# Query product of an attention layer on two float16 parts, with its weights read once more ahead for a scale, and all readings ahead rounded to bfloat16 by the transfer

## The chip, the cores and the metric

One core of a Trainium2 chip. The metric is the device time of one launch in microseconds (us); the kernel before was run three times, with a median of 1736.61 us (1736.53 to 1737.1).

## The reference

Two layers of a small diffusion transformer on 256 tokens x and 256 context tokens, width 2048, branch width 4096, all in float32. Layer 0 has a Fourier branch, layer 1 an attention branch. Cut to what matters here:

```python
def _attention_branch(h, hc, w_in, sink, rows, cols, need_ctx):
    q, k, v, z = jnp.split(h @ w_in, [D_BRANCH, D_BRANCH + kvw, D_BRANCH + 2 * kvw], axis=-1)
    kc, vc = jnp.split(hc @ w_in[:, D_BRANCH:D_BRANCH + 2 * kvw], 2, axis=-1)
    ...
    q = _axial_rope(q.reshape(b, n, ATTN_Q_HEADS, ATTN_HEAD_DIM), rows, cols)
    ...
    y = jnp.moveaxis(o, 0, 1).reshape(b, n, D_BRANCH) * jax.nn.silu(z)

for i in range(DEPTH):
    shift, scale, gate = jnp.split((jax.nn.silu(c) @ ada_w[i] + ada_b[i])[:, None, :], 3, axis=-1)
    h = _rmsnorm(x, norm_g[i]) * (1 + scale) + shift
    ...
    x = x + gate * (y @ w_out[i])
    if need_ctx:
        xc = xc + gate_c * (yc @ w_out[i])
return _rmsnorm(x, final_g)
```

The query product is the first 4096 columns of `h @ w_in`: 256 x 2048 by 2048 x 4096.

## The kernel before

**Products on two parts.** Every large product is made of three matmuls (mm3, L144 to L147): with w and x each split into a high and a low part, high times high, high times low, low times high. There are two ways of splitting a 128x1024 piece of weights. half_split (L69) rounds to the reduced fp32r on ACT (L66) and subtracts on DVE (L67); the parts are 4 bytes an element and take two slots of the pool ws. split16 (L134) multiplies by a power of two and rounds to float16 on ACT (L137) and forms the low part on DVE (L138); the parts share one slot of ws, but the scale must be known before the first piece is split, so that float16 does not overflow or lose its low bits.

**Readings ahead.** The scale of a weight matrix comes from the sum of its squares, so the matrix is read once ahead of the product that uses it. scan_loads (L831) reads layer 0's output weights wo0, scan_loads1 (L816) the key/value weights wkv and layer 1's output weights; loads2 in the key/value stage reads the rest of these. GpSimd (POOL) issues the loads, 128x512 float32 each into slots of the pool act (128x1024 into tiles pz in loads2); scan_sums (L826 to L829) squares them on ACT and adds the rows into a column of scn. half_scale, h1_bound and h1_scale turn the columns into power-of-two scales; h1_bound sends two columns through DRAM so that each partition gets the values of all.

**Stages, by the profile's time.** Opening and layer 0's Fourier product to about 326 us; layer 0's gate product to 657 (b = 0 to 31, 48 matmuls each); its output product to about 996 (i = 0 to 31, 48 matmuls of 128x512 each; step i first splits its two weight pieces, then issues readings, then goes on with the adaptive weights); key/value product 1002 to 1084; the query product, layer 1's gate product and attention, woven into each other by a list of units (emit_unit), to about 1590; layer 1's output product to the end. The query product takes the x half of the layer's input from hx1 (fp32r, two parts); the key/value product takes x and context from hz (float16, two parts).

**Order around the change.** Every engine works in the order of its instruction list. ada_jobs (L769 to L797) multiplies the adaptive-norm weights by a broadcast row: each step loads a tile zr on the queue of SP (L787) and a tile wa on POOL's queue (L790), and reduces each on DVE (L792). So a wa is issued behind the readings that stand ahead of it on POOL, and on DVE its reductions stand between the low parts (L138) of the output product's weights. In the output product ada_rate says how many of these steps go with step i, w_rate how many double readings of wkv and of layer 1's output weights.

Of the kernel before, what the change touches and what calls it, by code (L numbers as in the profile page):

```python
# [14 lines left out]
ALU = mybir.AluOpType  # L15
# [17 lines left out]
def tile_dit(ctx: ExitStack, tc: tile.TileContext, a: dict, out: bass.AP):  # L33
# [776 lines left out]
    ek, upk, dnk, kw = (keepc[:, c : c + 1] for c in range(4))  # L810
# [3 lines left out]
    scans1 = iter(range(52))  # L814

    def scan_loads1(n):  # L816
        for j in [next(scans1) for _ in range(n)]:
            for q in range(2):
                t = act()
                c = (j % 2 * 2 + q) * 512  # L820
                nc.gpsimd.dma_start(t, wst[j // 2][:, c : c + 512])
                c = j * 2 + q
                c += 80 if c < 28 else -28
                pend.append((t, scn[:, c : c + 1]))
# [6 lines left out]
    def scan_loads(n):  # L831
        for j in [next(scans) for _ in range(n)]:
            for q in range(2):
                t = act()
                c = (j % 2 * 2 + q) * 512
                nc.gpsimd.dma_start(t, a["wo0"][j // 32, j % 32 // 2][:, c : c + 512])
                c = j * 2 + q - 64 * (j >= 40)
                pend.append((t, scn[:, c : c + 1]))
# [5 lines left out]
    def half_sum(sw):  # L844
        return [col_sum(scn[:, sw * 16 : sw * 16 + 64])] + [col_sum(scn[:, 80:108])] * (sw == 0)
# [13 lines left out]
    with tc.tile_pool(name="yp", reuse_waits="tile", bufs=32) as ypool:  # L859
# [39 lines left out]
        if True:  # L899
# [44 lines left out]
            for b in range(4, NB):  # L944
# [28 lines left out]
                scan_loads((2 if b % 3 else 1) if b < 28 else 0)  # L973
            out0[0] = True
# [29 lines left out]
        hbd = dram.tile([P, 2], F32, name="hbd")  # L1004
        hb1 = []

        def h1_bound():
            m, c = h_bound(gs1, sh1, False), tiny(F32, 4, "t4")
            V.tensor_copy(c[:, 0:1], m)
            for i, q in ((2, slice(80, 108)), (3, slice(0, 4))):  # L1010
                V.tensor_reduce(c[:, i : i + 1], scn[:, q], axis=AX.X, op=ALU.add)
            V.tensor_tensor(c[:, 1:2], c[:, 2:3], c[:, 3:4], op=ALU.add)
            nc.gpsimd.dma_start(hbd, c[:, 0:2])
            hb1.append(act())
            nc.gpsimd.dma_start(hb1[0][:, 0:N], hbd.rearrange("(o p) c -> o (p c)", o=1).broadcast_to([P, N]))

        def h1_scale():
            v = hb1[0][:, 0:N].rearrange("p (n c) -> p c n", c=2)
# [7 lines left out]
            V.tensor_reduce(s, v[:, 1], axis=AX.X, op=ALU.add)  # L1026
            V.tensor_scalar(kw, s, 2.0**-70, None, op0=ALU.max)
            V.tensor_scalar(kw.bitcast(I32), kw.bitcast(I32), 24, 23, op0=ALU.logical_shift_right, op1=ALU.logical_shift_left)
# [798 lines left out]
```

## Time and profile before

| | before |
|---|---|
| median of three runs | 1736.61 us |
| the profiled execution's own time | 1736.42 us |
| its span, first to last instruction | 1734.6 us |
| HBM read / written | 419.30 MB / 12.59 MB |
| HBM traffic over the span | 249 GB/s |
| POOL's DMA queue (q0): packets, MB, share of 16 engines | 47344, 125.58, 22.7% |
| SP's DMA queue (q1): packets, MB, share of 16 engines | 197568, 335.60, 59.3% |
| mean granted TensorE clock | 0.998 |

How to read the profile: PE is TensorE's matmuls, PEld its weight loads (which overlap), DVE VectorE, ACT ScalarE, POOL GpSimd, SP the engine that issues most loads. In the row of slices each digit is the busy share in tenths of one fortieth of the span. A group is line, engine, operation, output<-inputs (partitions x elements, type), xcount | busy us, mean ns of one | idle time of the engine just before them and what ended it. A wait row names the waiting engine with its line, then what it waited for: us in total, times, the longest. Line numbers are those of the kernel of the profile.

### The profile page before, as it was taken

The numbers are of one execution on the slowest core, as the hardware profiler recorded it, in microseconds if no ns is written. First come the engines' busy times: TensorE is split into PE (matmuls) and PEld (weight loads), VectorE is DVE, ScalarE is ACT, GpSimd is POOL, SyncE is SP. The second block draws the span as 40 slices with busy tenths as digits, with TensorE's granted clock in tenths as the row PEclk, the third lists the DMA queues.
The fourth block names the chain that finished last, engine by engine and source line by source line (L and its number), as shares of the span: only waits on it lengthen the run. The fifth ranks groups of instructions, "written<-read, shape, count | busy, mean of one in ns | idle before, by whom it ended". The sixth has DMA issues, their size and how long they took to land. (4 is left out here: it accounts for less than half of the span.)

```text
span 1734.6 us, 28325 instructions
## 1 busy us (share of the span) xinstructions
PE 1703.1 (98%) x10379; PEld 1129.7 (65%) x10379; DVE 1373.2 (79%) x2390; ACT 1103.8 (64%) x2111; POOL 276.0 (16%) x429
## 2 busy tenths in 40 slices
PE   6999999999999999999999999999999999999997
PEld 4679999644444444446444654788888888876464
DVE  5779888798676787778689686888898989887755
ACT  5545555477777765464435397777787778777643
POOL 0001111211221204301420121300000000050001
PEclk9999999999999999999999999999999999999999
DMA  9998999869898968985997497489989899988643
GB/s 393 417 362 257 273 272 268 308 246 330 323 305 306 324 243 331 395 302 221 363 358 277 149 341 253 146 198 224 258 229 212 235 237 236 227 220 290 218 170 121
DMA packets 249195, 469.94 MB, mean 271 GB/s; under 512 B 171392, under 2 KB 171792, under 8 KB 222176
## 3 DMA queue, kind: packets, MB, share of 16 engines
q1 hardware_dynamic: 197568, 335.60, 59.3%
q0 software_dynamic: 47344, 125.58, 22.7%
q10 hardware_dynamic: 4144, 6.95, 1.2%
q8 instruction: 81, 1.33, 0.3%
q14 instruction: 58, 0.48, 0.1%
HBM read 419.30 MB, written 12.59 MB: 249 GB/s over the span
## 5 line engine op out<-in xcount | busy, mean ns | idle before, releaser
L67 DVE TENSOR_TENSOR wl<-raw,wh 128x1024 fp32r<-128x1024 f32 x152 | 188.4, 1256 | 43.1 <-ACT wh L66 33.0
L146 PE MATMUL ps<-act,wf 128*128 128x512 f16 x512 | 194.0, 379 | 0.0
L66 ACT CAST wh<-raw 128x1024 fp32r<-128x1024 f32 x152 | 157.3, 1046 | 57.6 <-PE ps L146 38.2
L147 PE MATMUL ps<-act,wf 128*128 128x512 f16 x512 | 191.1, 379 | 0.0
L145 PE MATMUL ps<-act,wf 128*128 128x512 f16 x512 | 189.8, 379 | 0.6 <-ACT wf L137 0.2
L145 PE MATMUL ps<-y,wf 128*128 128x512 f16 x448 | 169.8, 379 | 0.8 <-ACT wf L137 0.8
L146 PE MATMUL ps<-y,wf 128*128 128x512 f16 x448 | 169.8, 379 | 0.0
L145 PEld LDWEIGHTS <-wf 128*128 128x128 f16 x960 | 93.7, 98 | 113.4 <-ACT wf L137 4.2
L147 PEld LDWEIGHTS <-wf 128*128 128x128 f16 x960 | 93.9, 98 | 113.1
L147 PE MATMUL ps<-y,wf 128*128 128x512 f16 x448 | 164.9, 379 | 0.0
L146 PEld LDWEIGHTS <-wf 128*128 128x128 f16 x960 | 93.9, 98 | 109.0
L137 ACT ACTIVATE wf<-raw,nrm 128x1024 f16<-128x1024 f32 x56 | 63.5, 1145 | 131.4 <-PE ps L147 74.5
L145 PE MATMUL ps<-h,wh 128*128 128x256 f32 x512 | 144.4, 282 | 0.0
L146 PE MATMUL ps<-h,wh 128*128 128x256 f32 x512 | 142.7, 279 | 0.0
L147 PE MATMUL ps<-h,wl 128*128 128x256 f32 x512 | 142.6, 279 | 0.0
L1506 ACT ACTIVATE p<-ps,mx 128x512 f32<-128x512 f32 x128 | 87.8, 687 | 67.1 <-DVE mx L1502 64.7
L138 DVE SCALAR_TENSOR_TENSOR wf<-raw,tn,wf 128x1024 f16<-128x1024 f32 x64 | 79.8, 1282 | 42.6 <-ACT wf L137 42.6
L829 ACT ACTIVATE act<-act 128x512 f32<-128x512 f32 x178 | 109.4, 616 | 5.7 <-DMA act<-in_wo 4.4
L146 PE MATMUL ps<-wl,h 128*128 128x512 f32 x256 | 101.4, 396 | 0.0
L147 PE MATMUL ps<-wh,h 128*128 128x512 f32 x256 | 101.2, 395 | 0.0
L145 PEld LDWEIGHTS ps<-h,wh 128*128 128x128 f32 x512 | 96.1, 188 | 7.1 <-issue 5.5
L145 PE MATMUL ps<-wh,h 128*128 128x512 f32 x256 | 100.0, 402 | 0.0
(430 smaller groups left out, 4645.0 us busy)
## 6 DMA issues: line engine op xcount, KB each, us to landing
raw<-in_wz SPq DMA_DIRECT2D x64, 1024.0 KB, 6.3
raw<-in_awp SPq DMA_DIRECT2D x32, 1024.0 KB, 12.7
zr<-in_adw SPq DMA_DIRECT2D x64, 512.0 KB, 6.7
wa<-in_adw POOLq DMA_DIRECT2D x64, 512.0 KB, 6.3
act<-in_wo POOLq DMA_DIRECT2D x128, 256.0 KB, 7.4
raw<-in_wo SPq DMA_DIRECT2D x32, 1024.0 KB, 8.2
raw<-in_wq SPq DMA_DIRECT2D x32, 1024.0 KB, 5.8
raw<-in_wu SPq DMA_DIRECT2D x32, 1016.0 KB, 7.1
```

The lines of the kernel that those rows point to most:

```text
L66: last_cast[0] = S.copy(h, src).ins
L67: last_sub[0] = eng.tensor_tensor(l, src, h.bitcast(F32), op=ALU.subtract).ins
L137: last_cast[0] = S.activation(w[:, 0], src, AF.Copy, scale=up).ins
L138: last_sub[0] = V.scalar_tensor_tensor(w[:, 1], src, up, w[:, 0], op0=ALU.mult, op1=ALU.subtract).ins
L145: PE.matmul(o, wh, xh, start=start, stop=False)
L146: PE.matmul(o, wh, xl, start=False, stop=False)
L147: return PE.matmul(o, wl, xh, start=False, stop=stop).ins
L829: S.activation(t, t, AF.Square, accum_out=c)
L1506: S.activation(pt[hh, tb], so[hh, tb], AF.Exp, bias=mx[:, hh, tb : tb + 1], scale=-1.0, accum_out=sm[:, hh, tb : tb + 1])
```

## The change

The query product gets split16 with a scale upq, and the float16 parts hz as its input instead of hx1 (which stays for layer 1's gate product). The x half of hz therefore moves to eight tiles hzx of the pool act that live until the last query unit. The scale dnq that undoes upq is put into the Squares of the norm of q and into the rope table. For upq the query weights wq are read once more ahead, 64 loads of 128x1024: scan_loadsq issues one with each b from 4 to 27 and two with b = 28 to 31 of the gate product (32), and the others in the output product by q_rate. And every reading ahead now is one load of 128x1024 into a bfloat16 tile sn; source and destination differ in type, so the transfer rounds. Of wo0 and wkv that is half as many loads as before, each of twice the source. The diff's core:

```diff
+    qsn = c32.rearrange("p k c -> p (k c)")[:, 0:64]
+
+    def scan_load(src, j, col):
+        t = actp.tile([P, 1024], BF16, tag="act", name="sn")
+        c = j % 2 * 1024
+        nc.gpsimd.dma_start(t, src[:, c : c + 1024])
+        pend.append((t, col))
+
+    def scan_loadsq(n):
+        for j in [next(scansq) for _ in range(n)]:
+            scan_load(a["wq"][j // 8, j // 2 % 4], j, qsn[:, j : j + 1])
 
     def scan_loads1(n):
         for j in [next(scans1) for _ in range(n)]:
-            for q in range(2):
-                t = act()
-                c = (j % 2 * 2 + q) * 512
-                nc.gpsimd.dma_start(t, wst[j // 2][:, c : c + 512])
...
+            c = j + 64
+            scan_load(wst[j // 2], j, scn[:, c : c + 1])
...
     def scan_loads(n):
         for j in [next(scans) for _ in range(n)]:
-            for q in range(2):
-                t = act()
-                c = (j % 2 * 2 + q) * 512
-                nc.gpsimd.dma_start(t, a["wo0"][j // 32, j % 32 // 2][:, c : c + 512])
...
+            scan_load(a["wo0"][j // 32, j % 32 // 2], j, scn[:, j : j + 1])
...
                 scan_loads((2 if b % 3 else 1) if b < 28 else 0)
+                scan_loadsq(1 if b < 28 else 2)
...
+        q_rate = {**{i: 2 for i in range(6)}, **{i: 1 for i in (10, 11, 12, 13, 17, 18, 19, 20, 21, 23, 25)}, **{i: 3 for i in (14, 15, 16)}}
-        hbd = dram.tile([P, 2], F32, name="hbd")
+        hbd = dram.tile([P, 3], F32, name="hbd")
...
+            V.tensor_reduce(c[:, 2:3], qsn, axis=AX.X, op=ALU.add)
...
+            for c, up_, dn_ in ((1, upk, dnk), (2, upq, dnq)):
...
             scan_loads1(w_rate.get(i, 0))
+            scan_loadsq(q_rate.get(i, 0))
...
-                z2 = kvp.tile([P, 1024], F16, tag="hz", name="hz", bufs=16)
+                if k % 2 == 0:
+                    zx.append(actp.tile([P, 1024], F16, tag="act", name="hzx"))
+                z2 = zx[k // 2][:, k % 2 * 512 : k % 2 * 512 + 512], kvp.tile([P, 512], F16, tag="hz", name="hz", bufs=16)
...
-                    t = kvp.tile([P, 1024], F32, tag="pz", name="pz", bufs=4)
+                    t = kvp.tile([P, 1024], BF16, tag="pz", name="pz", bufs=8)
...
+                        V.tensor_scalar(rope, rope, dnq, None, op0=ALU.mult)
...
-                    S.activation(act(), oq[tb], AF.Square, accum_out=sq[:, tb, 0:1])
+                    S.activation(act(), oq[tb], AF.Square, scale=dnq, accum_out=sq[:, tb, 0:1])
...
-                return half_split(raws1[src], i % 2)
+                return split16(raws1[src], i % 2, upq) if kind == "q" else half_split(raws1[src], i % 2)
...
-                            pe_last[0] = mm3(o[tb], hx1[k][:, tb * P : (tb + 1) * P], hx1[k][:, N + tb * P : N + (tb + 1) * P], wh[:, q], wl[:, q], k == 0, k == KT - 1)
+                            t = hz[k][0]
+                            pe_last[0] = mm3(o[tb], t[:, tb * P : (tb + 1) * P], t[:, N + tb * P : N + (tb + 1) * P], wh[:, q], wl[:, q], k == 0, k == KT - 1)
```

The first place is POOL's list at the start of layer 0's output product, between two loads of wa (the adaptive weights, in_adw); in_wo is layer 0's output weight, x2 means twice in a row. Before:

```order
L790 DMA wa<-in_adw 128x1024 x5
L836 DMA act<-in_wo 128x512 x21
L790 DMA wa<-in_adw 128x1024
L836 DMA act<-in_wo 128x512 x9
L790 DMA wa<-in_adw 128x1024
L836 DMA act<-in_wo 128x512 x6
L821 DMA act<-in_wkv 128x512 x2
L836 DMA act<-in_wo 128x512 x4
L821 DMA act<-in_wkv 128x512
L790 DMA wa<-in_adw 128x1024
```

And in the changed kernel, behind the wa that is the last of the five above (in_wq is the query weight):

```order
L790 DMA wa<-in_adw 128x1024
L821 DMA sn<-in_wq 128x1024 x2
L821 DMA sn<-in_wo 128x1024 x2
L821 DMA sn<-in_wq 128x1024 x2
L821 DMA sn<-in_wo 128x1024 x2
L821 DMA sn<-in_wq 128x1024 x2
```

The pairs go on so up to the next wa. Between the two wa stand 21 loads in both kernels, of 256 KB before and of 512 KB of source now, 11 of them of wq.

The second place follows in the changed kernel: behind nine more loads and a wa, the eleven loads and the two blocks of xT (the tokens, to which the product is added) ahead of the next wa. There stood 13 loads of 128x512 before (the 6, 2, 4 and 1 above), and the two xT came behind that wa and the next:

```order
L790 DMA wa<-in_adw 128x1024
L821 DMA sn<-in_wo 128x1024 x2
L821 DMA sn<-in_wkv 128x1024
L821 DMA sn<-in_wq 128x1024
L821 DMA sn<-in_wo 128x1024 x2
L821 DMA sn<-in_wkv 128x1024
L821 DMA sn<-in_wq 128x1024
L821 DMA sn<-in_wo 128x1024 x2
L821 DMA sn<-in_wq 128x1024
L1066 DMA act<-in_xT 128x512 x2
L790 DMA wa<-in_adw 128x1024
```

After three more loads in both kernels comes the wa whose reductions stand in the third place; from the first wa to it there are 46 readings before, 44 in the changed kernel.

The third place is DVE at step i = 7 of the output product: the reductions of zr and wa (ISA rows) and the low part wf of the step's weights. In the changed kernel:

```order
L792 ISA zr_7630,acc_4144<-zr_7630,cb_6331 128x1024
L792 ISA acc_4144 128x1
L792 ISA junk_4143,acc_4144<-wa_7634,cb_6331 128x1024
L792 ISA acc_4144 128x1
L138 SCALAR_TENSOR_TENSOR wf_7768<-raw_7766,nrm_101,wf_7768 128x1024
L792 ISA wa_7634,acc_4144<-wa_7634,cb_6331 128x1024
```

Nothing moved on DVE here: before, the same rows stand in the same order (with other buffer numbers), wf directly behind the first reduction of the second wa.

41 lines of the change are left out of this document (18 added, 23 removed).

## The prediction

> **What bounds the kernel now.** I read the page's busy shares and slices first, then what PE waits for, then each stage by itself.
>
> ```profile
> PE 1703.1 (98%) x10379; PEld 1129.7 (65%) x10379; DVE 1373.2 (79%) x2390; ACT 1103.8 (64%) x2111; POOL 276.0 (16%) x429
> PE   6999999999999999999999999999999999999997
> DMA  9998999869898968985997497489989899988643
> ```
>
> PE is busy 98% of the span, and in all slices but the first and the last. So a stage is as long as its matmuls; another engine or a transfer costs time only where it makes PE wait. The waits of PE from 1085 to 1600 us (the query stage and attention), then from 330 to 1085 us:
>
> ```profile
> PE ps L146 <- DVE wl L67: 1.5, 2, 1.1
> PE ps L145 <- ACT wh L66: 0.5, 1, 0.5
> PE ps L145 <- ACT wf L137: 0.9, 2, 0.8
> ```
>
> That is 2 us of waiting for weights in 515 us, and 0.9 us in the 755 us ahead of it. How much cover there is shows in the stretches (length, then busy PE, PEld, DVE, ACT, POOL, then clock, DMA share, GB/s): layer 0's gate product, its output product, and two parts of the query and attention stage.
>
> ```profile
> 370.00:660.00 290.00, 290.00 (x1393) 132.11 (x1392) 227.17 (x401) 211.50 (x446) 58.69 (x111) 1.00 0.85 302
> 660.00:957.00 297.00, 296.23 (x1368) 142.16 (x1367) 233.56 (x355) 146.22 (x290) 75.54 (x142) 1.00 0.86 324
> 1112.00:1350.00 238.00, 237.06 (x1762) 196.22 (x1762) 212.60 (x394) 184.64 (x360) 12.14 (x9) 1.00 0.91 225
> 1350.00:1500.00 150.00, 150.00 (x1133) 124.93 (x1130) 133.10 (x253) 114.62 (x230) 4.66 (x4) 1.00 0.90 228
> ```
>
> The granted clock is 1.00 everywhere. The first two stretches are where the change adds reading, and their DMA engines are 85 and 86% busy already; the third and fourth are where the query product changes, with DVE 89% busy in both.
>
> **The query product (the gain).** Its matmuls are these three groups, 256 each, 768 together:
>
> ```profile
> L146 PE MATMUL ps<-wl,h 128*128 128x512 f32 x256 | 101.4, 396 | 0.0
> L147 PE MATMUL ps<-wh,h 128*128 128x512 f32 x256 | 101.2, 395 | 0.0
> L145 PE MATMUL ps<-wh,h 128*128 128x512 f32 x256 | 100.0, 402 | 0.0
> ```
>
> Matmuls overlap, so the price of one is the distance of their starts, not the 396 ns. From the timeline (start, duration), two rows 33 matmuls apart in the query product, and two rows 20 matmuls apart in the key/value product, which has the form that the query product gets (two float16 parts, 512 columns):
>
> ```profile
> 1180.10 0.40 PE L146 MATMUL ps<-wl,h 128*128 128x512 f32 x1
> 1187.80 0.40 PE L146 MATMUL ps<-wl,h 128*128 128x512 f32 x1
> ...
> 1039.63 0.38 PE L146 MATMUL ps<-wf,hz 128*128 128x512 f16 x1
> 1043.95 0.38 PE L145 MATMUL ps<-wf,hz 128*128 128x512 f16 x1
> ```
>
> 7.70/33 = 0.2333 us against 4.32/20 = 0.2160 us. The count of matmuls stays at three a pair, so the gain is 768 × 0.0173 = **13.3 us**. It is there only if the split keeps up: 64 pieces go from half_split to split16.
>
> ```profile
> L66 ACT CAST wh<-raw 128x1024 fp32r<-128x1024 f32 x152 | 157.3, 1046 | 57.6 <-PE ps L146 38.2 <-PE ps L147 12.1 <-DVE acc L792 3.9
> L137 ACT ACTIVATE wf<-raw,adab 128x1024 f16<-128x1024 f32 x50 | 56.1, 1141 | 34.9 <-PE ps L147 15.5 <-PE ps L146 10.1 <-DMA raw<-in_wo1b 3.4
> L67 DVE TENSOR_TENSOR wl<-raw,wh 128x1024 fp32r<-128x1024 f32 x152 | 188.4, 1256 | 43.1 <-ACT wh L66 33.0 <-issue 5.9 <-PE ps L147 2.7
> L138 DVE SCALAR_TENSOR_TENSOR wf<-raw,adab,wf 128x1024 f16<-128x1024 f32 x50 | 67.2, 1363 | 27.3 <-ACT wf L137 27.3
> ```
>
> ACT gets 64 × 95 ns = 6.1 us more, DVE 64 × 107 ns = 6.8 us. DVE's 345.7 of 388 us in the two stretches become 352.5 in some 375, or 94%: under the end, so I cost the split at nothing, with the rest as a rival. One weight slot instead of two for each piece lets the split run further ahead, which speaks for this. The scale on the Squares, one multiplication of the rope table (128x256) and five one-column steps of the scale are a dozen short instructions off PE's way: nothing.
>
> **The readings on ACT.** A reading of 128x512 costs ACT one Square; for the 128x1024 form I take the nearest row, a Square of that size that writes bfloat16.
>
> ```profile
> L829 ACT ACTIVATE act<-act 128x512 f32<-128x512 f32 x178 | 109.4, 616 | 5.7 <-DMA act<-in_wo 4.4 <-DMA act<-in_wkv 1.3
> L81 ACT ACTIVATE sq<-raw 128x1024 bf16<-128x1024 f32 x52 | 54.2, 1046 | 0.0
> ```
>
> Gate product: 80 readings become 72 long ones, 72 × 1.046 − 80 × 0.616 = +26 us, so ACT goes from 211.5 to about 238 of 290. Output product: 98 become 81, +24 us, 146 to 170 of 297. Both fit, cost nothing.
>
> **The readings on the DMA queues (the loss).** POOL issues fewer of them (178 become 153 of all), each of twice the source: a row of 4096 bytes is read and 2048 are written. The trace of before has no transfer that changes the type, so its price must be bounded. By the bytes written it is that of the old 256-KB load, by the bytes read twice that, and by read and written together three times. The place where it decides is the start of the output product, where the DMA engines are full (10-us stretches, same columns):
>
> ```profile
> 658.00:668.00 10.00, 10.00 (x48) 4.51 (x46) 9.56 (x15) 5.31 (x13) 6.77 (x13) 1.00 0.86 311
> 668.00:678.00 10.00, 10.00 (x48) 4.55 (x47) 7.96 (x10) 10.00 (x23) 4.98 (x10) 1.00 1.02 388
> 678.00:688.00 10.00, 10.00 (x48) 4.56 (x47) 2.06 (x3) 1.70 (x3) 2.68 (x5) 1.00 1.02 392
> 688.00:698.00 10.00, 10.00 (x48) 4.48 (x46) 7.92 (x12) 5.97 (x12) 6.96 (x13) 1.00 0.95 320
> 698.00:708.00 10.00, 10.00 (x48) 4.55 (x47) 8.95 (x13) 5.97 (x12) 4.69 (x9) 1.00 1.03 404
> 708.00:718.00 10.00, 10.00 (x48) 4.57 (x47) 4.15 (x6) 4.83 (x11) 2.83 (x6) 1.00 1.02 402
> 718.00:728.00 10.00, 10.00 (x48) 4.51 (x46) 8.67 (x14) 3.73 (x7) 3.93 (x8) 1.00 1.02 396
> ...
> 771.00:781.00 10.00, 10.00 (x48) 4.58 (x47) 3.78 (x4) 7.84 (x16) 0.53 (x1) 1.00 0.51 182
> 781.00:791.00 10.00, 10.00 (x48) 4.52 (x47) 9.91 (x17) 5.97 (x12) 3.15 (x6) 1.00 0.32 96
> ```
>
> A full share moves about 402 GB/s. POOL's queue takes the readings and the adaptive weights wa in order, and DVE works in order: its reduction of wa (L792) stands ahead of the low part wf (L138) that PE needs. Step i of the output product is 48 matmuls, 48 × 0.2157 = 10.35 us, from the 657.9 of the first row below. On DVE:
>
> ```profile
> L145 PE MATMUL ps<-y,wf x448: 379/379/389, 657.9 to 970.2; 128*128 128x512 f16 x150
> ...
> 723.96 1.23 DVE L792 CUSTOM_DVE_ANT_0 junk<-wa,cb 128x1024 f32<-128x1024 f32 x1 [1.26 <-DMA wa<-in_adw]
> 725.11 0.08 DVE L792 DVE_READ_ACCUMULATOR2_ANT acc<- 128x1 f32 x1
> 725.11 1.28 DVE L138 SCALAR_TENSOR_TENSOR wf<-raw,nrm,wf 128x1024 f16<-128x1024 f32 x1
> ```
>
> This wf belongs to the first half of i=7, which PE reaches at 657.9 + 7 × 10.35 = 730.3; it is done at 726.4. The slack is 4 us, and the wa ahead of it was late already (DVE idled 1.26 us). From 658 us to that wa POOL issues 46 readings before and 44 after (its two orders are shown with the change), and after also two xT blocks of 256 KB that before came later. By bytes read: 44 × 0.524 − 46 × 0.262 + 0.52 = 11.5 MB more, or 28.7 us at 402 GB/s. Of this, 1.9 us fit into the unused share of the first and fourth of these stretches, and 4 us into the slack: PE stalls **22.8 us** between i=4 and i=7. By bytes written the sum is 44 × 0.262 − 46 × 0.262 + 0.52 = 0 MB, and no stall. By both together it is 23.1 MB, 57.4 us, and a stall of 51.5 us. In every load of before as much is read as written, so these rows can't tell the sides apart. I take the bytes read: a conversion has to fetch all of the row, and a transfer whose fetching side is as long as in the full-share rows has no reason there to be shorter. The other two are kept for the range. A fourth bound is the one transfer that computes on its way, the accumulation into the Fourier weights, from 125.5 to 129.5 us:
>
> ```profile
> q0 software_dynamic: 1040, 0.52, 110.3%
> ```
>
> 1.103 × 4 us × 16 engines / 1040 = 68 ns for 508 bytes, so 0.55 us for a row of 4096 and 4.4 us for a load; 153 of them would cost 670 us of all engines. I give that little weight, because an accumulation also reads what it adds to.
>
> The later readings cost nothing by this price: 37 after i=7 instead of 52 are 5.8 MB more, 14 us, and the stretches from 771 to 791 alone leave 11.7 us free, with 14% of the whole stage (41 us of 297) unused. The 27 of the key/value stage read what they read before. The gate product gets 72 × 0.524 − 80 × 0.262 = 16.8 MB more, 58 GB/s over its 290 us: 302 become 360, under 402. Its engines get 41.7 us more on 246.5 busy, 288 of 290 at worst; thin, but the readings are not needed in their own step.
>
> [...]
>
> **The sum.** The profiled execution took 1736.4 us (span 1734.6 and 1.8 around it), 0.2 under the median of 1736.61. 1736.4 − 13.3 + 22.8 = 1745.9, so **1746 us**.
>
> **The rivals.** *Written bytes set the price (faster).* Then a reading is as dear as before, no wa is late, and the gain stands: 1736.4 − 13.3 = 1723, up to 1732 with smaller waits. It decides between the two prices at the point where 44 loads bring no more than the 5.9 us that fit: 0.353 MB-equivalents a load, two thirds of the read price. For it speaks that nothing in the trace puts the 402 GB/s on the reading side; against it, that nothing puts it on the writing side, where the bytes are halved. [...]
>
> *A dearer conversion (slower).* With read and written bytes added, 51.5 us of stall in the output product, and in the gate product 72 × 0.786 − 80 × 0.262 = 35.6 MB, 89 us on engines that are free for 43.5: some 45 more. That gives 1736.4 − 13.3 + 51.5 + 45 = 1820; 1760 to 1850.
>
> *The gain stays away.* If DVE at 94% becomes the end in the query stage (attention's DVE work comes in bursts), PE waits for wf as it now waits for wl, at most the 6.8 us added and the 13.3 won: 1730 to 1740, without a stall elsewhere.
>
> **How the numbers follow.** Late wa by read bytes, 1733 to 1756 around 1746: 0.41. Written bytes, 1723 to 1732: 0.37. Dearer conversion: 0.14. Gain lost without a stall: 0.08. Two outcomes of both signs hold most of the chance, so the range spans them: 1722 to 1765, which leaves out most of the dear case; the likeliest case's own range is 1733 to 1756. About 0.2%, 3.5 us, is what a measurement of this kernel tells from no change. Faster by more: the second case and a little of the last, 0.39. Within it: the low end of the first case (a stall of 10 to 17 us) and half of the last, 0.14. Slower: 0.47.
>
> **What the profile after would show.** Query matmuls 0.216 us apart: step one is right. On DVE in front of i=4 to i=7, idle time put down to wa of 10 us and more, PE waiting there for wf of L138, and the rows from 658 to 760 all at a share near 1.0: the loss is right. If a reading's packets take what 2048 bytes take, those rows look like before and the forecast is wrong towards 1723. If DMA is full from 370 on and PE waits in the gate product too, it is wrong upwards.

## The result and the profile after

| | before | after |
|---|---|---|
| median of four runs | 1736.57 us (1735.92 to 1737.1) | 1760.52 us (1758.82 to 1762.27) |
| ratio, 95% interval | | 1.0138 [1.0121, 1.0156] |
| profiled execution's own time, span | 1736.42, 1734.6 us | 1760.35, 1758.5 us |
| mean granted TensorE clock | 0.998 | 0.988 |
| HBM read | 419.30 MB | 452.92 MB |

The kernel is slower by 24 us. The forecast of 1746 us had the sign, and its range holds the time, but it took the loss for 9.5 us. From the page of after: the busy row of PE, the slices of PE, clock and DMA, and POOL's DMA queue.

```profile
PE 1701.4 (97%) x10379; PEld 1063.2 (60%) x10379; DVE 1378.7 (78%) x2395; ACT 1163.4 (66%) x2061; POOL 263.6 (15%) x404
...
PE   6999999999999999699999999999999999999997
...
PEclk9999999999999999899999999999999999999999
DMA  9998999789998989988998578359999999989643
...
q0 software_dynamic: 55152, 112.01, 27.4%
```

PE is busy for nearly as long as before, though its query matmuls got shorter. The seventeenth slice (703 to 747 us) holds a 6 where there was a 9, and there alone the clock shows an 8. What PE waited for in after, first from 326 to 1000 us, then the first two rows from 1000 us to the end:

```profile
PE ps L145 <- ACT wf L137: 11.6, 6, 8.3
PE ps L147 <- DVE wf L138: 7.0, 2, 4.3
...
PE ps L1400 <- ACT fq L1390: 3.0, 2, 2.7
PE ps L1255 <- ACT act L1246: 2.6, 1, 2.6
```

18.6 us of waiting for split weights, where before had 0.9, and two waits of 2.6 to 2.7 us in places where before had at most 0.4.

**Where the 24 us came from.** Both kernels run the same 10379 matmuls, in the same order but for a few places, so I compared their starts in the two traces where the orders agree. The growth of that shift, place by place, is the loss:

| place | forecast | measured |
|---|---|---|
| to the end of layer 0's gate product (657 us) | 0 | +0.1 |
| output product, i = 4 to 7 | +22.8 | +20.7 (6.1 at i = 5, 14.6 from there to the end of i = 7) |
| output product, i = 8 to 31, and the start of key/value | 0 | +4.6 (3.9 of it at i = 21) |
| key/value product, its end, with the first 130 query matmuls | −2.2 | +3.9 (2.2 won, 6.1 lost) |
| transposes of the first query head | 0 | +4.1 |
| query product and attention, the rest (638 query matmuls) | −11.1 | −10.9 (11.1 won, 0.2 lost) |
| layer 1's output product, from its first matmuls at 1561 us | 0 | +1.4 |
| sum | +9.5 | +23.9 |

What was won is the count of matmuls times the 0.0173 us of the prediction; run 3, without the loss at the end of key/value, confirms it there: its shift falls by 2.2 us.

**The forecast stall.** Stretches of after in the output product (columns as in the prediction; 48 matmuls are a full stretch):

```profile
670.00:680.00 10.00, 10.00 (x48) 4.48 (x46) 4.83 (x6) 8.54 (x15) 3.41 (x7) 1.00 1.12 228
...
710.00:720.00 10.00, 5.74 (x27) 2.46 (x26) 2.65 (x4) 5.31 (x10) 3.18 (x6) 1.00 1.09 268
720.00:730.00 10.00, 10.00 (x40) 4.16 (x39) 8.35 (x12) 1.39 (x2) 2.69 (x5) 0.83 1.09 287
730.00:740.00 10.00, 6.80 (x32) 2.89 (x30) 1.23 (x2) 0.00 (x0) 2.66 (x5) 1.00 1.06 334
740.00:750.00 10.00, 2.13 (x5) 0.56 (x6) 8.43 (x14) 5.49 (x7) 0.53 (x1) 0.54 0.95 289
```

The DMA share is 1.06 to 1.12 in the first four (packets that overlap in the profile are added up) while the GB/s, in which a converted packet counts with its written size (2048 bytes for a row of 4096), is 228 to 334. DVE is idle in the same stretches. Its timeline says for what (start, duration, then in brackets the idle time before and what ended it):

```profile
717.35 1.23 DVE L792 CUSTOM_DVE_ANT_0 junk<-wa,cb 128x1024 f32<-128x1024 f32 x1 [7.83 <-DMA wa<-in_adw]
...
741.39 1.23 DVE L792 CUSTOM_DVE_ANT_0 junk<-wa,cb 128x1024 f32<-128x1024 f32 x1 [9.58 <-DMA wa<-in_adw]
```

Those are the reductions of late wa that the prediction named, and the low part wf (L138) stands behind them. The wa are late since POOL's list holds them back. Its issues of wa in after, then in before (start, duration):

```profile
658.71 0.54 POOL L790 DMA_DIRECT2D wa<-in_adw  x1 [11.82 <-issue]
...
688.97 0.53 POOL L790 DMA_DIRECT2D wa<-in_adw  x1 [2.18 <-DMA sn<-in_wq]
```

```profile
658.59 0.53 POOL L790 DMA_DIRECT2D wa<-in_adw  x1 [12.70 <-issue]
...
679.45 0.53 POOL L790 DMA_DIRECT2D wa<-in_adw  x1 [1.86 <-DMA act<-in_wo]
```

21 loads stand between the two in both kernels. They now take 30.3 us instead of 20.9, since POOL goes on only as earlier loads land: from the ninth load on, each of these issues stands 0.28 to 0.54 us behind the landing of the eighth load ahead of it, in both traces. By the issue and landing times POOL never has more than eight loads in flight, in either kernel; its loads take turns on eight semaphores (111 to 118). So the bound in these two kernels is a count: eight readings are 2.1 MB of source before and 4.2 MB now, and whatever stands behind them in the list waits for that.

**A cost that was not in the sum.** PE's timeline of after, behind its longest stop:

```profile
745.14 0.61 PE L145 MATMUL ps<-y,wf 128*128 128x512 f16 x1 [8.34 <-ACT wf L137]
...
749.30 0.63 PE L145 MATMUL ps<-y,wf 128*128 128x512 f16 x1
...
753.57 0.63 PE L146 MATMUL ps<-y,wf 128*128 128x512 f16 x1
...
754.66 0.38 PE L146 MATMUL ps<-y,wf 128*128 128x512 f16 x1
754.87 0.38 PE L147 MATMUL ps<-y,wf 128*128 128x512 f16 x1
```

From the second to the third row are ten matmuls, 0.427 us each; the last two stand 0.21 apart. The granted clock fell to half while PE stood, at 740.8 us, and came back at 754.4, some 9 us behind the end of the stop. In the output product of after 30 matmuls ran like this, 8 behind the stop at 716, 15 behind those at 737 and 746, 7 behind one at 899: 30 × 0.211 = 6.3 us beside 18.6 us of waits, and the two make the delay of that stage (24.9).

### The profile page after: what moved, and what is told of

Read it like the earlier page. It is cut to its first block, busy times and chain, and to the rows that moved or that the text cites. A ratio compares the mean times of both kernels' runs of the same rounds, so it can differ in the third digit from the quotient of the medians.

```text
span 1758.5 us, 28196 instructions
## 1 busy us (share of the span) xinstructions
PE 1701.4 (97%) x10379; PEld 1063.2 (60%) x10379; DVE 1378.7 (78%) x2395; ACT 1163.4 (66%) x2061; POOL 263.6 (15%) x404
## 3 DMA queue, kind: packets, MB, share of 16 engines
HBM read 452.92 MB, written 12.59 MB: 265 GB/s over the span
## 5 line engine op out<-in xcount | busy, mean ns | idle before, releaser
L138 DVE SCALAR_TENSOR_TENSOR wf<-raw,adab,wf 128x1024 f16<-128x1024 f32 x114 | 157.3, 1390 | 55.2 <-ACT wf L137 55.1
L145 PE MATMUL ps<-y,wf 128*128 128x512 f16 x448 | 172.2, 385 | 11.1 <-ACT wf L137 11.1
L836 ACT ACTIVATE sn<-sn 128x1024 bf16<-128x1024 bf16 x153 | 159.9, 1047 | 12.6 <-DMA sn<-in_wq 10.1
L137 ACT ACTIVATE wf<-raw,adab 128x1024 f16<-128x1024 f32 x114 | 128.0, 1144 | 54.3 <-PE ps L147 24.0
L67 DVE TENSOR_TENSOR wl<-raw,wh 128x1024 fp32r<-128x1024 f32 x88 | 109.4, 1247 | 26.0 <-ACT wh L66 15.1
L145 PE MATMUL ps<-wf,hzx 128*128 128x512 f16 x320 | 122.1, 383 | 0.3 <-ACT hzx L1170 0.3
L146 PE MATMUL ps<-wf,hzx 128*128 128x512 f16 x320 | 121.8, 382 | 0.0
L147 PE MATMUL ps<-wf,hzx 128*128 128x512 f16 x320 | 120.8, 382 | 0.0
L138 DVE SCALAR_TENSOR_TENSOR wf<-raw,tn,wf 128x1024 f16<-128x1024 f32 x64 | 79.9, 1282 | 46.7 <-ACT wf L137 46.6
```

The source lines that it names most:

```text
L67: last_sub[0] = eng.tensor_tensor(l, src, h.bitcast(F32), op=ALU.subtract).ins
L137: last_cast[0] = S.activation(w[:, 0], src, AF.Copy, scale=up).ins
L138: last_sub[0] = V.scalar_tensor_tensor(w[:, 1], src, up, w[:, 0], op0=ALU.mult, op1=ALU.subtract).ins
L145: PE.matmul(o, wh, xh, start=start, stop=False)
L146: PE.matmul(o, wh, xl, start=False, stop=False)
L147: return PE.matmul(o, wl, xh, start=False, stop=stop).ins
```

## The experiments

The theory at this point was the forecast's: loads of twice the source put more bytes ahead of the wa. Open were which part brings the loss (the reading of wq, the bfloat16 tiles, or both), whether the price is on the reading side, and where the unforecast 14 us come from. Each kernel was timed beside the kernel before.

**1. The change without the reading of wq.** The sums of wq are a constant; no load of wq goes out.

```diff
-        for j in [next(scansq) for _ in range(n)]:
-            scan_load(a["wq"][j // 8, j // 2 % 4], j, qsn[:, j : j + 1])
+        if next(scansq) == 0:
+            nc.gpsimd.memset(qsn, 0.5)
```

> The changed kernel without the 64 readings of wq ahead; their sums are set to a constant 0.5 a column, which is what these weights give, so the scale stays. Theory A (the readings of wq make wa late at the start of the output product): the two stalls there, 20.8 and 4.2 us in the changed kernel, shrink to 4 us or less in all, the 7.5 us around the end of the key/value product and the 10 us won in the query stage stay: 1735 to 1739 us. Rival B (the conversion as such is what costs): the stall stays above 10 us, 1745 us or more.

Measured: 1752.6 us, 1.0087 [1.0066, 1.0107]. Stalls of 6.3 us at i = 5, 4.7 at i = 8 and 10.8 at i = 20 remain in the output product, and +5.5 at i = 31 and the start of key/value, +4.1 at the first head; the end of key/value shows no loss. So a kernel that reads no more than before, in bfloat16 tiles, still loses 22.4 us in the output product, where after loses 24.9. Without the wq bytes the first place (i = 4 to 8) loses 11.6 us instead of 20.7, but i = 20 loses more; over the stage they are not the main cause.

**2. The query product alone.** The kernel before with split16 for the query weights, the scale from a constant, no reading of wq, and readings in float32 as they were.

```diff
-                return half_split(raws1[src], i % 2)
+                return split16(raws1[src], i % 2, upq) if kind == "q" else half_split(raws1[src], i % 2)
...
+            V.memset(c[:, 2:3], 32.0)
```

> The query product of the change alone: split16 with a scale from a constant sum, no reading of wq, all other readings as before (float32, 128x512, four pz tiles). Theory A with theory C (the loss at the end of the key/value product comes from the bfloat16 pz tiles with eight buffers): no stall anywhere, only the gain: 10 to 13.3 us under before, 1723 to 1727 us. Rival D (that loss comes from the query pieces that split16 puts into ACT's and DVE's lists there): 7 us more, 1730 to 1734 us.

Measured: 1728.96 us, 0.9951 [0.9937, 0.9966]. Up to the key/value product nothing moves. The query stage wins 13.4 us, and one place gives 5.4 back, the transposes of the first query head. The row of the high part of the normed query (ACT) and the transposes that wait for it (PE) in this kernel, with two rows of DVE ahead of them, and the same ACT row in before:

```profile
1119.01 1.27 DVE L138 SCALAR_TENSOR_TENSOR wf<-raw,adab,wf 128x1024 f16<-128x1024 f32 x1
1120.20 0.15 DVE L1376 TENSOR_SCALAR sq<-sq 128x2 int32<-128x2 int32 x1
...
1120.39 1.33 ACT L1388 ACTIVATE fq<-act,sq 128x512 f16<-128x512 f32 x2 [3.32 <-DVE sq L1376]
...
1121.17 0.40 PE L1398 MATMUL ps<-ident,fq 128*128 128x128 f16 x4 [2.70 <-ACT fq L1388]
```

```profile
1118.98 1.34 ACT L1381 ACTIVATE fq<-act,sq 128x512 f16<-128x512 f32 x2 [0.67 <-DVE sq L1369]
```

The scale sq, a handful of columns on DVE, stands in DVE's list behind low parts of the next query weights (1.27 us each; 1.21 in before). It is done 1.4 us later than in before, while PE, with the shorter query matmuls behind it, comes there 1.8 us earlier. PE stops for 2.70 us, and behind that the granted clock is 0.5 for 6.8 us.

**3. The change with float32 tiles in the key/value stage.** All else as in the change.

```diff
-                    t = kvp.tile([P, 1024], BF16, tag="pz", name="pz", bufs=8)
+                    t = kvp.tile([P, 1024], F32, tag="pz", name="pz", bufs=4)
```

> The changed kernel with the readings of the key/value stage as before: float32 pz tiles, four buffers; nothing else undone. Theory C: the 7.5 us around the end of the key/value product go, 1753 us, with the output product's stalls unchanged. Rival D: within 1 us of the changed kernel, 1760 us.

Measured: 1757.1 us, 1.0108 [1.0091, 1.0125]. The 6.1 us at the end of key/value are gone, the stalls of the output product are nearly as in after, and PE no longer waits at L1255. The first head costs 5.3 us here instead of 4.1, so 3.4 us of the 6.1 show in the median. What stood there shows on ACT's timeline of after:

```profile
1075.10 1.04 ACT L1189 ACTIVATE pz<-pz 128x1024 bf16<-128x1024 bf16 x1
...
1082.37 1.05 ACT L1189 ACTIVATE pz<-pz 128x1024 bf16<-128x1024 bf16 x1
1083.41 0.90 ACT L1203 ACTIVATE h<-ht,sh 128x256 fp32r<-128x256 f32 x2
...
1113.20 0.63 ACT L1246 ACTIVATE act<-act 128x512 f32<-128x512 f32 x1 [2.37 <-DVE act L1143]
```

Eight Squares in a row, the eight bfloat16 tiles that fit where four fitted, stand ahead of the work that makes hx1; everything behind comes later, to the Squares (L1246) whose sums PE's L1255 needs. With four tiles the Squares come in ones and twos between that work. The block of eight alone is not enough: it stands in runs 1 and 4 too, and neither loses there. Run 1 has the new query product as well, but PE comes 2.8 us later (a shift of 28.2 us against 25.4) and the Squares of L1246 are 0.7 us earlier. So the block uses up the cover, and how early PE comes decides whether that costs; the second half of this is argued from the three traces.

**4. The bfloat16 readings alone.** The kernel before with every reading as one load of 128x1024 into a bfloat16 tile.

```diff
-            for q in range(2):
-                t = act()
-                c = (j % 2 * 2 + q) * 512
-                nc.gpsimd.dma_start(t, a["wo0"][j // 32, j % 32 // 2][:, c : c + 512])
...
+            scan_load(a["wo0"][j // 32, j % 32 // 2], j, scn[:, j : j + 1])
```

> The kernel before with all its readings as bfloat16 tiles of 128x1024 rounded by the transfer, and nothing else of the change. Theories A and C: at 1.38 us of all DMA engines a load instead of 2 x 0.64, some 2 to 4 us of stall in the output product, and 7 us around the end of the key/value product: 1743 to 1748 us. Rival B: a stall of 10 us and more in the output product, 1753 us or more. Rival D: no loss at the key/value product's end, 1737 to 1741 us.

Measured: 1756.83 us, 1.0113 [1.0091, 1.0134]; the profiled execution took 1753.06. Stalls of 5.4 us at i = 5 and 6 and of 10.9 at i = 20, with the same bytes of source as before. The second is in a region that the prediction took for free. POOL's and DVE's timelines of this kernel, then POOL's of before:

```profile
830.82 1.06 POOL L790 DMA_DIRECT2D wa<-in_adw  x2 [25.36 <-DVE gt L1040]
...
869.21 0.53 POOL L790 DMA_DIRECT2D wa<-in_adw  x1 [0.73 <-DMA sn<-in_wo1b]
...
878.73 1.23 DVE L792 CUSTOM_DVE_ANT_0 junk<-wa,cb 128x1024 f32<-128x1024 f32 x1 [23.25 <-DMA wa<-in_adw]
```

```profile
777.73 0.53 POOL L790 DMA_DIRECT2D wa<-in_adw  x1 [14.49 <-ACT y L895]
787.85 0.53 POOL L790 DMA_DIRECT2D wa<-in_adw  x1 [9.58 <-PE ps L147]
...
825.12 1.06 POOL L790 DMA_DIRECT2D wa<-in_adw  x2 [23.13 <-DVE gt L1046]
...
855.09 0.53 POOL L790 DMA_DIRECT2D wa<-in_adw  x1 [0.78 <-DMA act<-in_wkv]
```

In before POOL stands still for 14.5 and 9.6 us in front of two wa, at 778 and 788, and for 23 us in front of two more, at 825 (25 us at 831 in this kernel); these wait for other engines. So the idle DMA time of before from 771 to 791, and from 811 to 831 (share 0.42 and 0.35), was out of reach of all that stands in POOL's list behind them: it issued no load between 801.5 and 825.1 us. Then 22 loads of 256 KB go out before the next wa in before, and 19 of 512 KB here: 30.0 us and 38.4. DVE stands 23 us for that wa.

**5. Rounding without the larger load.** The kernel before, readings of 128x512 as before, into bfloat16 tiles in the gate and output products; the key/value stage is unchanged. POOL's list is nearly that of before.

```diff
-                t = act()
+                t = actp.tile([P, 512], BF16, tag="act", name="sn")
```

> The kernel before with its readings in z0's and the output product's stages still as 128x512 loads, but into bfloat16 tiles, rounded by the transfer; as many loads as before, in nearly the same places of POOL's list (key/value stage unchanged). Theory E (the loss of e4 comes from the list: the weights wa keep their place by number of loads, and each load ahead of them moves twice as much): a load costs 0.69 us of all engines instead of 0.64, 2 to 3 us more ahead of the wa at i=7 against 4 us of slack: 1735 to 1740 us. Rival B (the conversion itself is the cost): the stalls of 17 us stay, 1750 us or more.

Measured: 1747.88 us, 1.0058 [1.0041, 1.0075]. No stall from i = 4 to 7; 12.6 us at i = 20 to 22. So the stall at i = 5 comes from the list (twice the bytes of source a load), the one at i = 20 from the conversion itself, where no slack was. The price of the conversion: POOL's queue in a busy stretch of after (667 to 688 us), of before (661 to 679) and of this kernel (661 to 679), as packets, MB, share of 16 engines:

```profile
q0 software_dynamic: 1814, 3.30, 83.8%
```

```profile
q0 software_dynamic: 1422, 4.74, 71.2%
```

```profile
q0 software_dynamic: 2326, 2.52, 79.5%
```

In engine time that is 0.838 × 21 × 16 = 282 us in after, for 6.60 MB of source (twice the 3.30 written), and 205 us for 4.74 MB in before: 23.4 and 23.1 KB of source a microsecond. By written bytes it would be 11.7 and 23.1. In this kernel's stretch a plain wa (0.52 MB) is among the 2.52 MB; its converted packets alone took 196 us for 3.99 MB of source, 20.4 KB a microsecond. Single packets say the same: in after a row of 4096 bytes written as 2048 takes 172 to 173 ns. A plain packet of 4096 has a median of 159 ns in the stretch of before, with a mean of 175, and a median of 172 on SP's queue in the same stretch of after. A row of 2048 written as 1024 takes 96 to 98 in this kernel, and two such rows do not share a packet as they do without conversion (128 packets a load, 64 in before). So in these runs a reading cost what its source costs read plainly, or up to 9% more, and 13 to 23% more in the short form.

**6. Run 4 with the readings of a step queued behind its wa.** The readings of step i are issued only after the last wa of the steps before.

```diff
+            with tc.issue_after(wa_in[-1]):
+                if i < 14:
+                    scan_loads({6: 1, 7: 1, 8: 1, 9: 1}.get(i, 2))
+                scan_loads1(w_rate.get(i, 0))
```

> e4 (readings as 128x1024 bfloat16, nothing else of the change) with one difference: in the output product the readings of step i are queued on POOL behind the wa of step i-1, so that no more than some six of them stand in a row ahead of a wa (21 and 17 before). Same loads, same bytes, same conversion. Theory E: the stalls at i=5 and i=20 of e4 go, 1735 to 1741 us. Rival B: they stay, 1750 us or more.

Measured: 1748.43 us, 1.0061 [1.0046, 1.0076]. The stalls at i = 5 and i = 20 are gone; 10.2 us of stall stand at i = 14, 25 and 26 instead. By the medians 8 us of run 4's loss are won, by the two profiled executions 5. Order repairs the early places and passes the late bytes on to later ones.

**7. Run 2 with one stage more ahead of the first head** (first = 12 instead of 11).

> e2 (the query product alone) with 12 instead of 11 units of products ahead of the first scores, which puts one unit of 12 matmuls, 2.6 us, ahead of the transposes that waited for fq. Theory F (the query stage wins the full 13.3 us, and gives 5.4 back in one wait of 2.8 us for fq with the lower clock behind it): 1736.6 - 13.3 = 1723 to 1725 us. Rival G (the wait only moves to the next product, or the units are missed at the end): 1728 to 1730 us, as e2.

Measured: 1737.89 us, 1.001 [0.9999, 1.002]. The wait at the first head is gone, but every later unit stands one place off, and PE waits for wl and wh of layer 1's gate product instead (8.0 us by the view of waits). The gain is gone.

**8. The change, gated, with wq spread over the gate product's later steps and steps 26 and 27**, float32 in key/value and first = 12.

> The changed kernel, computing the same, with four edits: readings behind wa as in e6, the readings of wq spread by the free DMA time of each step (37 in the gate product, one for each of i=0 to 5, three for i=14 to 16, 26 and 27, and so on; those of wo1 at i=28 to 30), float32 tiles in the key/value stage as in e3, 12 units as in e7. Theories A, E and F together: no stall over 2 us is left, 1723 to 1728 us, faster than before. If the wq readings' bytes can't be hidden at all in the output product (64 x 1.38 = 88 us of engine time more than before over both stages): 1735 us or more.

Measured: 1749.2 us, 1.0067 [1.0052, 1.0082]. The output product loses only 9.0 us, at i = 14. The query stage loses its phase as in run 7.

**9. Run 7 with the phase kept.** One filler fewer in the first stage, and the slot counted on, so that only the first head gets more room.

```diff
-                filler(4 if b < 32 else 1)
+                filler((4 if b else 3) if b < 32 else 1)
...
+                slot[0] += not b
```

> e2 (the query product alone) with 12 units ahead of the first scores and 3 instead of 4 in the first stage behind them, so that only the transposes of the first head move by one unit and everything later keeps its place (in e7 all later stages moved by one unit and waited for weights). Theory F (full 13.3 us in the query stage, given back in one wait for fq of 2.8 us and the lower clock behind it): 1723 to 1725 us. Rival G: 1728 us or more, as e2 or e7.

Measured: 1724.55 us, 0.9926 [0.9911, 0.9941], against 1738.36 us in its own runs of before. The wait at the first head in PE's view of waits:

```profile
PE ps L1398 <- DVE fq L1389: 0.5, 2, 0.3
```

It was 2.7 us at once in run 2. By the medians the query product without that loss wins 13.8 us; before, timed beside it, stands 1.8 us above its 1736.6 of most other runs, against which it would be 12. That is near the forecast 13.3. The profiled execution, at 1727.16 us the slowest of the four, still waits 1.7 us more for split weights than before does. The kernel beats both others, but its scale is a constant that holds for these weights; it reads nothing ahead to prove it.

**10 and 11. The change with the three repairs together.** Gating, 40 pieces of wq in the gate product and 24 in the output product, float32 in key/value, the first head as in run 9; run 10 with bfloat16 tiles, run 11 with pairs of 128x512 float32.

```diff
-                scan_loadsq(1 if b < 28 else 2)
+                scan_loadsq(2 if b >= 28 or b % 3 == 0 else 1)
...
-        w_rate = {10: 1, 11: 1, 14: 2, 15: 2, 16: 2, 17: 1, 18: 1, 20: 1, 22: 2, 24: 3, 26: 3, 27: 3, 28: 3}
...
+        w_rate = {10: 1, 11: 1, 14: 2, 15: 2, 16: 2, 17: 1, 18: 1, 20: 1, 22: 2, 24: 3, 28: 3, 29: 3, 30: 3}
+        q_rate = {**{i: 1 for i in (*range(6), 12, 13, 19, 21, 23, 25)}, **{i: 2 for i in (14, 15, 16)}, 26: 3, 27: 3}
```

> The changed kernel, computing the same, with: readings queued behind the wa of the step before, readings of wq spread (40 in the gate product, 24 in the output product, at most two a step ahead of i=26), float32 tiles in the key/value stage, and the units as in e9. Theory: out0 loses under 5 us, the key/value stage nothing, the query stage wins 13: 1724 to 1730 us. If the converting loads keep the DMA queues too full in the output product: 1733 us or more.

> e10 with all readings as pairs of 128x512 float32 loads, as before: the same sources read, no conversion, 1.27 instead of 1.38 us of all DMA engines a piece, twice as many tiles. If the conversion's 9% decides where the queues are full: 3 to 8 us under e10, 1722 to 1726 us. If only the bytes read matter: the same as e10 within 2 us. If ACT (128 more Squares of 0.62 us, 82 us in all, most in the gate product) becomes the end there: 1735 us or more.

Measured: 1740.14 us, 1.001 [1.0001, 1.0019], and 1740.94 us, 1.0012 [1.0002, 1.0022]. With all repairs the change is still not faster; it stands within 0.2% of before. Run 10 still loses 13 us in the output product in stops of 0.6 to 3.3 us; run 11 loses nothing until one stop at i = 16, PE's longest in its view of waits:

```profile
PE ps L145 <- ACT wf L137: 14.8, 2, 14.7
```

**12. The change with pairs of float32 loads in its places.** Nothing is rounded; the pieces of wq stand where the change has them.

> The changed kernel, computing the same, with all readings (those of wq too, at their places) as pairs of 128x512 float32 loads into two tiles each, and float32 tiles in the key/value stage; no readings queued behind wa, nothing spread otherwise. POOL's list then holds 24 loads of 256 KB between the two wa at the start of the output product, where the changed kernel holds 21 of 512 KB. Theory H (the bfloat16 tiles cost twice over: each load is 9% dearer by the conversion, and one tile instead of two lets the list put twice the bytes ahead of a wa): the stalls of 20.6 us at i=5 to 7 shrink to under 8 us, 1730 to 1742 us. Rival A (the bytes of the wq readings themselves are what is too much there): the stalls stay above 15 us, 1748 us or more.

Measured: 1761.22 us, 1.0146 [1.0108, 1.0184], so the change is as slow without any rounding. But the loss sits elsewhere: at i = 5 to 7 nothing (after: 20.7), then 1.9 us at i = 10 and 11, 12.2 at i = 16, 4.2 at i = 24 to 26, 5.8 at i = 30 and 6 at the start of key/value. From the first wa of the stage to the fourth behind it, the one that the prediction priced, POOL issues 53 loads of 256 KB here, 13.9 MB by 719 us; in after 44 readings of 512 KB and two of xT, 23.6 MB by 737; in before 46 of 256 KB, 12.1 MB by 710. Loads of twice the source, counted one for one, put more bytes ahead of the wa; that a bfloat16 tile takes one slot where the pair takes two is why the list can hold them so, which is argued from the lists.

**13 and 14. Two more placements of run 11.** Run 13 takes wq out of i = 14 to 16; run 14 puts 50 of the 64 pieces into the gate product, without gating, and moves adaptive steps from i = 12 and 13 to 26 and 27.

> e11 with no reading of wq at i=14 to 16 (the six pieces go to i=10 and 11 and to four steps of the gate product); computes the same as the changed kernel. Theory H: e11's one stall (16.4 us at i=16, where ACT's list held readings that landed late ahead of the weights' split) goes, and nothing else is left: 1723 to 1728 us, faster than both kernels. If the bytes of the readings are too much for the output product in any order: 1735 us or more.

> e13 without the queueing behind wa, with 50 of the 64 wq pieces read in the gate product (100 float32 loads), 14 in the output product (one each at i=0 to 5, 10 to 13, 19, 21, 23 and 25), the wo1 readings back at i=26 to 28, and the adaptive steps of i=12 and 13 moved to i=26 and 27, so that DVE's list at i=16 holds no reductions between the evictions and the scale; computes the same as the changed kernel. If e11's and e13's stall at i=16 (16 and 14 us) came from those reductions in the chain of the second scale (theory I): it goes, 1723 to 1729 us. If it came from the bytes of the wq readings: it stays, 1735 us or more. If the gate product is too full with 50 pieces (some 275 of its 290 us of DMA and of ACT): a new stall ahead of 657 us.

Measured: 1742.81 us, 1.0036 [1.0025, 1.0047], and 1747.78 us, 1.0073 [1.0053, 1.0093]. The profiled execution of run 13 took 1750.85 us, 8 over its median; in it 13.8 us stand at i = 16, 7.4 at i = 31 and the start of key/value, and 2.3 in the gate product. Run 14 turns the gate product itself into a stage that waits (9.2 us), and its output product loses 14.5 more, 5.9 of it at i = 7 to 11 and 7.2 at i = 16. A stretch of it in the gate product:

```profile
450.00:530.00 80.00, 78.50 (x378) 35.60 (x377) 55.23 (x100) 72.68 (x172) 29.98 (x56) 1.00 0.99 380
```

The DMA share is 0.99 and ACT 91% busy. The 33.6 MB of wq found no free place in any of the placements tried. For the stop at i = 16 the lists of run 11 suggest that late reductions stand on DVE among the steps of the second weight half's scale. In run 14, where the adaptive steps of i = 12 and 13 come later, none stands between the evictions and the scale, and 7.2 us stay of 16.4. So they are at most a part of it; the run changes more than that, and the rest stays open.

## Why the prediction was right in sign and short in size

The gain and the stall came near their terms. The step that failed is the one that put all other places at nothing. The missing 14.4 us are mostly these: the later readings (4.6), the end of key/value (6.1) and the first query head (4.1). The slow clock behind stops (6.3, inside the stall and the later readings) stood in no term either.

**The query product: right.** Matmuls of the query product in after, 21 apart on PE's timeline:

```profile
1203.65 0.38 PE L147 MATMUL ps<-wf,hzx 128*128 128x512 f16 x1
...
1208.18 0.38 PE L147 MATMUL ps<-wf,hzx 128*128 128x512 f16 x1
```

4.53 / 21 = 0.2157 us, where the key/value rows gave 0.2160. The stage wins 13.4 us gross in run 2 against a term of 13.3. The rival that DVE becomes the end fell: DVE is 92% busy in this stage of after and PE keeps its pace.

**The gate product: right.** 288 of 290 us of DMA time were worked out as worst case. The stretch of after, with a shift of 0.1 us:

```profile
370.00:657.00 287.00, 287.00 (x1379) 130.64 (x1378) 224.29 (x396) 234.19 (x421) 52.05 (x98) 1.00 0.98 295
```

The share is 0.98, ACT is busy 234 us of 287 where 238 of 290 were forecast, and a reading on ACT takes the 1.046 us that was read from the other Square:

```profile
L836 ACT ACTIVATE sn<-sn 128x1024 bf16<-128x1024 bf16 x153 | 159.9, 1047 | 12.6 <-DMA sn<-in_wq 10.1
```

Run 14 shows how thin the cover was: 18 pieces more, with all readings as plain float32 pairs, cost 9.2 us there.

**The stall at i = 4 to 7: mechanism and place right, size near partly by luck.** 20.7 us instead of 22.8, but of other parts: 15.3 of stop (4.3, 8.3 and 2.7), nearly all the rest slow clock, which stood in no term. The wa that the sum priced landed 22.5 us later than in before (746.4 against 723.9), where the sum gives 26.8. PE did not first stand for that one: the two wa ahead of it landed at 717.3 and 741.4, 18.5 and 23.6 us later than in before, and stopped DVE at i = 5 and i = 7. The price by bytes read, which the prediction took without being able to see it, is borne out by run 5; the measured one lies 0 to 9% above it. The rival by written bytes is refuted, and so is the sum of both sides. Two workings of these rivals do not come out: counted alike for the old loads, both sides together would be one and a half old loads and not three, where two were measured (1.38 us of all engines against 0.64 to 0.69); and 5.9 us at 402 GB/s are 2.4 MB, so the border between the prices lies at 0.316 MB a load and not at 0.353. By the rival the row with half the bytes written would have been the cheaper one; it took 172 ns, read as 4096 and written as 2048 bytes, against 159 to 172 plain.

**"The later readings cost nothing by this price": the step that failed.** It compared bytes with the DMA engines' idle share over the stage. But readings are issued in the order of POOL's list, and in the idle stretches that list stands behind a wa that waits for another engine (14.5, 9.6 and 23 us in before). What counted in these runs is the bytes between two wa, and there the time had no slack: 3.9 us at i = 21 in after, 10.8 and 10.9 at i = 20 in runs 1 and 4. In after the same place costs less, as the earlier stalls have already moved PE back; that the stalls trade in this way is argued from the three runs, not isolated.

**The 27 of key/value that "read what they read before": failed, 6.1 us.** The bytes are the same, but the tile is half as large, and twice as many Squares go ahead in a block on ACT (run 3), which costs where PE comes early enough (run 1). The prediction counted the cost on the queue and left out the order on the engine that consumes.

**The split at nothing, "a dozen short instructions off PE's way": failed, 4.1 us.** DVE has the time; its list does not have the order. The short chain that frees the first head's transposes stands behind low parts of 1.27 us (run 2), and putting room there without shifting the other stages gets it back (run 9).

**What was in no term.** Behind four of the stops in the output product the granted clock was 0.5, which added about a third to the waits there (6.3 us on 18.6). In layer 1's output product 1.4 us are lost: waits of 0.8 and 1.1 us for split weights at 1567 and 1569 are followed by 3.4 us of half clock, and 0.6 us come behind the last matmul; why is not traced. All these together, 4.6 + 6.1 + 4.1 + 1.4 us and 0.3 elsewhere, less the 2.1 by which the forecast stall was too large, make the 14.4 us between the forecast and the measured time.

## What to carry to other kernels

When a load gets larger or its tile smaller, count the bytes that the issuing engine's list can now put ahead of the next transfer that someone waits for (here at most eight loads in flight, of 256 KB as of 512 KB of source); here the mean share of the DMA engines, 0.86 of the stage, said nothing on that, and their idle time in front of a blocked list (POOL stood 14.5, 9.6 and 23 us) was not to be had. A smaller tile can also change how far the consumer runs ahead, and so the order of work on its engine (eight Squares in a row on ACT in after, ones and twos with four tiles). Reading 34 MB more, in stages whose DMA engines were 85 and 86% busy, ate a gain of some 13 us in every placement that was tried.

## What the runs showed of the hardware

**Behind some stops of PE its clock was half for a while, behind others not.** Stops of 2.83 and 2.92 us (run 5) were followed by 7 matmuls at 0.43 us (the second with a further stop of 1.83 us close behind), 2.70 us (run 2) by 11, 3.59 us (run 6) by 13, 4.26 us (after) by 8; stops of 2.38 us (run 6) and of 2.57 and 3.02 us (run 10) by none, and one of 2.00 us in after, with one of 0.15 us 5 us ahead, by 7. So in these runs a stop of 2.4 to 3 us cost 0 to 2.3 us on top of itself, and the one of 3.59 us 2.8. In the trace of after the stretches at a granted clock of 0.5 that end inside the kernel last 3.41, 13.65 and 3.41 us in the output product, from 720.3, 740.8 and 901.2 us on, and 6.83, 3.41 and 3.41 us from 1112.8, 1153.8 and 1570.2 us on: once, twice or four times 3.41 us. What decides whether such a stretch follows a stop of 2 to 3 us was not shown.

**The converting transfers cost what they read, or more.** 172 to 173 ns for a row of 4096 bytes written as 2048, 96 to 98 ns for 2048 written as 1024 (run 5), against medians of 159 (before) and 172 ns (after) for a plain packet of 4096 bytes. Halving the written bytes saved nothing, and rows of 2048 bytes that share a packet when copied plainly each took one of their own (128 packets a load in run 5, 64 in before).
